# Gate-matrix operands in blocks of 8 tokens, one step ahead of their matmuls, and other rates for the gathered steps

## The chip, the core and the metric

The kernel runs on one core of a Trainium2 chip. A core has TensorE (PE in the rows), VectorE (DVE), ScalarE (ACT), GpSimd (POOL) and SyncE (SP), each with its own instruction queue, and DMA engines for moving data. The metric is the device time of one execution in microseconds, the median of several runs. A time inside the trace is counted from the start of the profiled span.

## The reference

One layer over 1024 tokens of width 1024: attention and mLSTM heads, then the product-key expert layer (PEER), then a gated projection and a norm. What matters here is PEER:

```python
# per token: 8 heads, each takes the 16 best of 128 x 128 experts
s = einsum('thcd,hcnd->thcn', q, sub_keys)          # scores of two halves of a key
sv, si = top_k(s, 16)                               # per half
cand = sv[..., 0, :, None] + sv[..., 1, None, :]    # 16 x 16 sums
top_s, pos = top_k(cand, 16); eidx = i * 128 + j    # of the chosen
g = softmax(top_s)
a = gelu(einsum('td,thkd->thk', x, expert_u[eidx]))
x = x + einsum('thk,thkd->td', g * a, expert_v[eidx])
# then, per token
x = x + sigmoid(rms_norm(x) @ w_ple_gate) * (p @ w_ple_proj);  out = rms_norm(x)
```

## The kernel before

The 1024 tokens are 8 tiles of 128. The kernel has four stretches: a front part (attention, mLSTM, projections and the choice of experts, to 974 us), dense_up (to 2009), dense_down (to 2932) and the tail (to 3122).

PEER is done in two ways. Tiles 0 to 2 fetch the rows of their 128 experts per token: `sparse` (L831) yields 400 steps, of which most hold a `u_step` (a gather of 512 KB by POOL at L827, then one VectorE multiply and sum, ru, L843) and a `v_step` (a gather of 512 KB and one VectorE addition onto ya, L861). After the last one of a tile, SP stores ya to x3_s (L865). `pump(x)` (L212) adds x to what is due and takes that many steps: `UP_RATE` says how many per column of dense_up (0.9 up to column 40, 1.45 from there), `DOWN_RATE` how many per row of dense_down (1.05, times a group of 4 rows), `TAIL_RATE` 8 at two places of each tail tile. A step's instructions get a lower priority than their surroundings, and each is kept behind the last VectorE operation that `anchor` (L201) has noted.

The other five tiles are done densely, against all 16384 experts. `dense_up` (L944) runs over 128 columns j: a table block of expert_u (raw, 512 KB) is split by ScalarE into thi and by VectorE into tlo (L881), TensorE makes A (L145), ScalarE ga (L992), which is stored to ga_s. `dense_down` (L1005) runs over 128 rows m in groups of four: it loads gq from g_s (L1049) and aq from ga_s (L1050), multiplies them (L1058), splits the product into ph and pl, and adds ph, pl times thi, tlo of expert_v into two kept PSUM banks (keep) and others (Y).

Between them stand the gates: `gate_blocks` (L891) makes, for the dense tiles, the 128 x 128 matrix of gate weights of each token as a product of two one-hot matrices, o0 (which first index) and o1 or w0 (which second index, times the weight in a high and a low part). For 16 tokens VectorE makes o1 (L918), w0 (L919), the low part in o1 (L920) and o0 (L921); for each 8 of them ScalarE copies w0 and o1 into wc in another order (L927), TensorE does 16 matmuls into pg (L931), ScalarE copies two pg into st (L934). For 32 tokens st, 2 MB, is stored to g_s (L938). The generator yields after each 8 tokens, 80 times in all. dense_up takes its steps (L999) from about column 42 on, at a pace that ends near column 119, and takes what is left after the last column (L1002). o0, o1, w0 and wc have one buffer each.

The tail (L1111) takes the tiles in the order 4, 0, 5, 6, 7, 1, 3, 2. A tile of 0 to 2 first pumps until its gathered sum is stored, then loads it as x (L1124), which TensorE transposes (L1139).

## Time and profile before

| | us |
|---|---|
| median of 3 runs | 3117.79 |
| lowest and highest run | 3115.04, 3124.81 |
| the profiled execution | 3123.69 |
| its span in the trace | 3121.9 |
| TensorE busy in the span | 2873.4 (92%) |
| VectorE busy in the span | 2557.4 (82%) |
| ScalarE, POOL busy in the span | 1317.8, 1007.6 |

In the rows of a later section, L12 is line 12 of the kernel before. "out<-in" gives the program's names of what an instruction writes and reads; o stands for o0 and o1, w for w0. An arrow in brackets says how long the engine was idle before, and what ended that. The granted clock is a share of TensorE's full speed. An instruction's duration in a row runs until its writes are done, and the next one of the same engine can start a little before that, so the cost of one instruction in a row of them is the distance between two starts.

### The profile page before, as it was taken

What the parts mean: (1) busy time and instruction counts of PE and PEld (TensorE: products, weight loads), DVE (VectorE), ACT (ScalarE), POOL (GpSimd) and SP (SyncE); (2) the same over time, 40 slices, a digit from 0 to 9 for tenths busy, and PEclk for the clock granted to TensorE, in tenths of its full rate; (3) what the DMA queues carried; (4) which work ended last, traced back from release to release, by engine and by line L of the source; (5) the groups of instructions that cost most, each with busy time, mean ns of one, the idle gap of its engine ahead of it and who ended that gap; (6) DMA issues with size and microseconds to landing.
All of it is one profiled execution on the core that took longest, in us unless ns stands there. A gap on an engine that the chain in (4) does not pass through costs nothing.

```text
span 3121.9 us, 44819 instructions
## 1 busy us (share of the span) xinstructions
PE 2873.4 (92%) x16367; PEld 2517.4 (81%) x16367; DVE 2557.4 (82%) x5349; ACT 1317.8 (42%) x2152; POOL 1007.6 (32%) x786
## 2 busy tenths in 40 slices
PE   7999989998697999999999999899989999998894
PEld 6887868776586999998889999778768888887773
DVE  5565889888799889799999797678778888888795
ACT  5664336655222222487776565212222222232241
POOL 0000000334414333444444555434333444414431
PEclk9999989999898999999999999899999999999997
DMA  5333433777846787899999989999989999988763
GB/s 168 100 111 127 150 126 93 233 229 244 303 133 233 264 276 244 306 345 340 343 340 346 370 328 367 372 348 340 313 291 330 339 333 329 338 295 276 259 222 124
DMA packets 316797, 829.01 MB, mean 266 GB/s; under 512 B 26144, under 2 KB 115104, under 8 KB 314016
## 3 DMA queue, kind: packets, MB, share of 16 engines
q0 software_dynamic: 112608, 410.04, 37.6%
q1 hardware_dynamic: 185536, 374.16, 34.9%
q10 hardware_dynamic: 18432, 41.95, 3.5%
q8 instruction: 128, 2.10, 0.3%
q14 instruction: 93, 0.76, 0.1%
HBM read 715.43 MB, written 102.24 MB: 262 GB/s over the span
## 4 chain that ended last, share of the span: by engine, by line
PE 55%; DVE 15%; DMA 12%; issue 12%; ACT 3%; POOL 2%; another core or an unknown queue 0%; SPq 0%; DVEq 0%; ACTq 0%; POOLq 0%
PE A L145 23%; PE mm L145 12%; PE keep L145 5%; DMA raw<-in_vr 4%; DMA rv<-in_ev,eidx 3%; DVE ya L861 3%; PE S L145 2%; DVE ru L843 2%; PE pg L931 2%; PE Y L136 2%; PE Y L137 2%; PE Y L138 2%; DVE tlo L881 1%; DMA ru<-in_eu,eidx 1%; POOL ru L827 1%
## 5 line engine op out<-in xcount | busy, mean ns | idle before, releaser
L827 POOL DMA_INDIRECT ru<-in_eu,eidx x384 | 508.4, 1324 | 1169.7 <-DVE ru L843 843.0
L827 POOL DMA_INDIRECT rv<-in_ev,eidx x384 | 491.2, 1279 | 443.5 <-DVE ya L861 286.8
L861 DVE SCALAR_TENSOR_TENSOR ya<-rv,cf,ya 128x1024 f32<-128x1024 f32 x384 | 492.3, 1282 | 46.5 <-DMA rv<-in_ev,eidx 29.3
L843 DVE SCALAR_TENSOR_TENSOR ru<-ru,sh 128x1024 f32<-128x1024 f32 x384 | 468.1, 1220 | 33.5 <-DMA ru<-in_eu,eidx 23.1
L881 DVE TENSOR_TENSOR tlo<-raw,thi 128x1024 fp32r<-128x1024 f32 x256 | 312.6, 1221 | 220.4 <-ACT thi L880 130.4
L880 ACT ACTIVATE thi<-raw 128x1024 fp32r<-128x1024 f32 x256 | 267.7, 1057 | 524.5 <-DMA raw<-in_vr 272.6
L145 PE MATMUL A<-ahi,thi 128*128 128x384 f32 x1024 | 348.7, 341 | 13.2 <-ACT thi L880 13.2
L145 PE MATMUL A<-alo,thi 128*128 128x384 f32 x1024 | 345.8, 338 | 0.0
L145 PE MATMUL mm<-ahi,whi 128*128 128x512 f32 (+1 forms) x752 | 301.4, 405 | 25.0 <-ACT ahi L236 13.1
L145 PE MATMUL mm<-alo,whi 128*128 128x512 f32 (+1 forms) x752 | 287.1, 394 | 7.1 <-DVE alo L237 7.1
L136 PE MATMUL Y<-thi,ph 128*128 128x512 f32 x640 | 250.2, 391 | 5.1 <-ACT thi L880 5.0
L145 PE MATMUL A<-xh,thi 128*128 128x256 f32 x1024 | 252.8, 284 | 0.7 <-ACT xh L971 0.7
L145 PE MATMUL A<-xl,thi 128*128 128x256 f32 x1024 | 252.7, 284 | 0.1
L137 PE MATMUL Y<-tlo,ph 128*128 128x512 f32 x640 | 250.0, 391 | 1.1 <-DVE tlo L881 1.0
L138 PE MATMUL Y<-thi,pl 128*128 128x512 f32 x640 | 249.4, 390 | 0.0
L1059 ACT ACTIVATE ph<-aq 128x640 fp32r<-128x640 f32 x128 | 87.3, 727 | 328.5 <-PE Y L137 309.4
L145 PEld LDWEIGHTS A<-ahi,thi 128*128 128x128 f32 x1024 | 193.6, 189 | 13.5 <-ACT thi L880 13.5
L145 PE MATMUL A<-ahi,tlo 128*128 128x384 f32 x1024 | 203.3, 337 | 0.0
L145 PE MATMUL keep<-tlo,ph 128*128 128x512 f32 x640 | 178.6, 403 | 22.7 <-DVE tlo L881 22.6
L145 PE MATMUL mm<-ahi,wlo 128*128 128x512 f32 (+1 forms) x752 | 193.9, 389 | 5.1 <-DVE wlo L196 5.0
L145 PEld LDWEIGHTS A<-xh,thi 128*128 128x128 f32 x1024 | 194.5, 190 | 1.0 <-ACT xh L971 0.9
L145 PEld LDWEIGHTS A<-xl,thi 128*128 128x128 f32 x1024 | 194.7, 190 | 0.3 <-DVE xl L972 0.3
(467 smaller groups left out, 6080.6 us busy)
## 6 DMA issues: line engine op xcount, KB each, us to landing
raw<-in_ut SPq DMA_DIRECT2D x128, 512.0 KB
raw<-in_vr SPq DMA_DIRECT2D x128, 512.0 KB
ga_s<-ga ACTq DMA_DIRECT2D x128, 320.0 KB
g_s<-st SPq DMA_DIRECT2D x20, 2048.0 KB
gq<-g_s SPq DMA_DIRECT2D x32, 1280.0 KB
aq<-ga_s SPq DMA_DIRECT2D x32, 1280.0 KB
wraw<-in_win SPq DMA_DIRECT2D x58, 512.0 KB
wraw<-in_wq SPq DMA_DIRECT2D x32, 512.0 KB
```

The costliest lines, as they stand in the source:

```text
L136: pe.matmul(o, lh, rh, start=start, stop=False)
L137: pe.matmul(o, lh, rl, start=False, stop=False)
L138: pe.matmul(o, ll, rh, start=False, stop=stop)
L145: pe.matmul(o, ll if p == "l" else lh, rl if p == "r" else rh, start=start and p == "h", stop=stop and n == last and p == names[-1])
L827: gp.indirect_dma_start(out=b, out_offset=None, in_=table, in_offset=bass.IndirectOffsetOnAxis(ap=eidx[part][:, i, k:k + 1], axis=0))
L843: behind(v.scalar_tensor_tensor(b, b, 1.0, st["h", tl], op0=OP.mult, op1=OP.mult, accum_out=st["d", n][:, j:j + 1]))
L861: op = v.scalar_tensor_tensor(ya, b, st["c", n][:, j:j + 1], ya, op0=OP.mult, op1=OP.add)
L880: sc.activation(hi, raw, AF.Copy)
L881: anchor(v.tensor_sub(lo, raw, hi.bitcast(F32)))
L931: pe.matmul(pg[:, b, :], o0[:, 4 * a + b, :], wc[:, c, a % 2, b, :], start=c == 0, stop=c == 1)
L1059: sc.activation(ph, av, AF.Copy)
```

## The change

Three numbers of the pace: `UP_RATE` takes 1.2 steps for each of the first 40 columns in place of 0.9, `DOWN_RATE` 1.1 in place of 1.05. And the gates: operands are made for 8 tokens at a time (o0, o1, w0 and each of the four VectorE operations have half the size), o0 and wc have two buffers, o1 and w0 still one. The matmuls, the copies to st and the store to g_s are in a function `gate_products`, which the generator calls for the operands of the step before, after it has emitted the operands of the current step. The last call stands behind the loop over tokens.

```diff
-UP_RATE = (0.9, 1.45, 40)
+UP_RATE = (1.2, 1.45, 40)
 QUIET = 5
-DOWN_RATE = 1.05
+DOWN_RATE = 1.1
...
-        sh = [P, 4, P, 4]
+        sh = [P, 2, P, 4]
         io = ioe[:, None].to_broadcast(sh)
+        prepared, held = [], {}
+
+        def gate_products(n, hb, sb, o0, wc):
+            if sb == 0:
+                held["st"] = gp_.tile([P, P, GB], F32, name="st", bufs=64 // GB)
+            st = held["st"]
+            for a in range(2):
+                pg = pG.tile([P, 4, P], F32, name="pg")
+                for b in range(4):
+                    for c in range(2):
+                        pe.matmul(pg[:, b, :], o0[:, 4 * a + b, :], wc[:, c, a, b, :], start=c == 0,
+                                  stop=c == 1)
+                t_ = sb * 8 + a * 4
+                sc.activation(st[:, :, t_:t_ + 4].rearrange("p j t -> p t j"), pg, AF.Copy, scale=1.0 / WSC)
+            if sb == GB // 8 - 1:
+                sy.dma_start(g_s[n * (P // GB) + hb], st)
+
...
-                st = gp_.tile([P, P, GB], F32, name="st", bufs=64 // GB)
-                for sb in range(GB // 16):
-                    tb = slice(hb * GB + sb * 16, hb * GB + sb * 16 + 16)
+                for sb in range(GB // 8):
+                    tb = slice(hb * GB + sb * 8, hb * GB + sb * 8 + 8)
...
-                    o0 = gp_.tile([P, 16, P], F16, name="o0", bufs=1)
+                    o0 = gp_.tile([P, 8, P], F16, name="o0", bufs=2)
                     o1 = gp_.tile(sh, F16, name="o1", bufs=1)
                     w0 = gp_.tile(sh, F16, name="w0", bufs=1)
-                    v.tensor_tensor(o1, iv[1], io, op=OP.is_equal)
-                    v.tensor_tensor(w0, o1, iv[2], op=OP.mult)
-                    v.tensor_tensor(o1, o1, iv[3], op=OP.mult)
-                    v.tensor_tensor(o0, it[:, 0, tb][:, :, None].to_broadcast([P, 16, P]),
-                                    ioe[:, None, :, 0].to_broadcast([P, 16, P]), op=OP.is_equal)
-                    for a in range(4):
-                        if a % 2 == 0:
-                            wc = gp_.tile([P, 2, 2, 4, P], F16, name="wc", bufs=1)
-                            for c, w in enumerate((w0, o1)):
-                                sc.activation(wc[:, c], w[:, a:a + 2].rearrange("p a j b -> p a b j"), AF.Copy)
...
-                        if a % 2:
-                            yield True
-                sy.dma_start(g_s[n * (P // GB) + hb], st)
+                    wc = gp_.tile([P, 2, 2, 4, P], F16, name="wc", bufs=2)
+                    v.tensor_tensor(o1, iv[0], io, op=OP.is_equal)
+                    v.tensor_tensor(w0, o1, iv[1], op=OP.mult)
+                    v.tensor_tensor(o1, o1, iv[2], op=OP.mult)
+                    for c, w in enumerate((w0, o1)):
+                        sc.activation(wc[:, c], w.rearrange("p a j b -> p a b j"), AF.Copy)
+                    v.tensor_tensor(o0, it[:, 0, tb][:, :, None].to_broadcast([P, 8, P]),
+                                    ioe[:, None, :, 0].to_broadcast([P, 8, P]), op=OP.is_equal)
+                    if prepared:
+                        gate_products(*prepared.pop())
+                    prepared.append((n, hb, sb, o0, wc))
+                    yield True
+        gate_products(*prepared.pop())
```

In the changed code the VectorE operations of a step are L935 (o1), L936 (w0), L937 (low part) and L940 (o0), the ScalarE copies to wc L939, the matmuls L907, the copies to st L910 and the store L912; gq and aq are loaded at L1057 and L1058.

VectorE within the gate stretch, in the order of the kernel before: from one block of 16 tokens to the next.

```order
L918 TENSOR_TENSOR o_15042<-it,ioe 128x2048
L921 TENSOR_TENSOR o_15041<-it,ioe 128x2048
L919 TENSOR_TENSOR w_15043<-o_15042,it 128x2048
L881 TENSOR_TENSOR tlo<-raw,thi 128x1024
L920 TENSOR_TENSOR o_15042<-o_15042,it 128x2048
L851 TENSOR_TENSOR cf<-cf,gsm_4438 128x16
L843 SCALAR_TENSOR_TENSOR ru,dots<-ru,sh_14973 128x1024
L861 SCALAR_TENSOR_TENSOR ya<-rv,cf,ya 128x1024 x2
L881 TENSOR_TENSOR tlo<-raw,thi 128x1024
L843 SCALAR_TENSOR_TENSOR ru,dots<-ru,sh_14973 128x1024
L918 TENSOR_TENSOR o_15298<-it,ioe 128x2048
```

The same place of the changed kernel: from one block of 8 tokens to the next, and the start of a third.

```order
L935 TENSOR_TENSOR o_14743<-it,ioe 128x1024
L940 TENSOR_TENSOR o_14837<-it,ioe 128x1024
L936 TENSOR_TENSOR w_14744<-o_14743,it 128x1024
L881 TENSOR_TENSOR tlo<-raw,thi 128x1024
L937 TENSOR_TENSOR o_14743<-o_14743,it 128x1024
L843 SCALAR_TENSOR_TENSOR ru,dots<-ru,sh_14405 128x1024
L861 SCALAR_TENSOR_TENSOR ya<-rv,cf,ya 128x1024
L935 TENSOR_TENSOR o_14838<-it,ioe 128x1024
L940 TENSOR_TENSOR o_15014<-it,ioe 128x1024
L936 TENSOR_TENSOR w_14839<-o_14838,it 128x1024
L843 SCALAR_TENSOR_TENSOR ru,dots<-ru,sh_14405 128x1024
```

Four operations of 2048 elements with eight others around them have become twice as many of 1024 elements, with fewer others in between: between the last use of o1 (L937) and its next writing (L935) stand two operations, where before L920 and L918 were six apart.

SP at the end of dense_up and the start of dense_down, before.

```order
L938 DMA g_s<-st 128x4096
L879 DMA raw<-in_ut 128x1024 x5
L938 DMA g_s<-st 128x4096
L879 DMA raw<-in_ut 128x1024 x4
L1049 DMA gq_20985<-g_s 128x20x128
L1050 DMA aq_20986<-ga_s 128x4x640
L879 DMA raw<-in_vr 128x1024 x2
L1049 DMA gq_20967<-g_s 128x20x128
```

The same place in the changed kernel.

```order
L912 DMA g_s<-st 128x4096
L879 DMA raw<-in_ut 128x1024 x8
L912 DMA g_s<-st 128x4096
L1057 DMA gq_21337<-g_s 128x20x128
L1058 DMA aq_21338<-ga_s 128x4x640
L879 DMA raw<-in_vr 128x1024 x2
L1057 DMA gq_21319<-g_s 128x20x128
```

The last store to g_s has moved from ahead of the last four loads of in_ut to a place behind them, directly ahead of the first gq.

VectorE near the end of the tail, before: the last ya, with the beginning of the last tile behind them (r_m, r_i and r_u are steps of its norm).

```order
L861 SCALAR_TENSOR_TENSOR ya<-rv,cf,ya 128x1024
L1182 SCALAR_TENSOR_TENSOR yac<-yac,r_u,gfin 128x512 x2
L861 SCALAR_TENSOR_TENSOR ya<-rv,cf,ya 128x1024 x5
L118 TENSOR_SCALAR r_m<-ss 128x1
L121 TENSOR_SCALAR r_m<-ss 128x1
L119 TENSOR_SCALAR r_i<-r_m 128x1
L120 TENSOR_SCALAR r_u<-r_i 128x1
L131 SCALAR_TENSOR_TENSOR r_h<-r_u,r_m 128x1
L1142 TENSOR_TENSOR al<-tr,ah 128x512
```

The last ya in the changed kernel, in the middle of another tile's work (yac and x are two tiles' outputs).

```order
L1182 TENSOR_TENSOR gt<-gt,pr 128x512
L1181 TENSOR_SCALAR gt<-gt 128x512
L1183 TENSOR_TENSOR x_28204<-gt,x_28204 128x512
L1182 TENSOR_TENSOR gt<-gt,pr 128x512
L861 SCALAR_TENSOR_TENSOR ya<-rv,cf,ya 128x1024
L1183 TENSOR_TENSOR x_28204<-gt,x_28204 128x512
L118 TENSOR_SCALAR r_m<-ss 128x1
L121 TENSOR_SCALAR r_m<-ss 128x1
L861 SCALAR_TENSOR_TENSOR ya<-rv,cf,ya 128x1024
L1186 TENSOR_TENSOR st_28337<-s_28325 128x1
L119 TENSOR_SCALAR r_i<-r_m 128x1
```

The last ya stands 184 rows ahead of the end there, before the last three tiles of the tail.

Over longer stretches of VectorE's order: by the end of column 40, 101 ru and 85 ya stand there before and 113 and 97 after; by the last tlo of dense_down 362 and 346 of 384 each before, 380 and 364 after. Between the tlo of columns 44 and 80 are 96 operations of the gates and 104 gathered ones before, 192 and 101 after; TensorE's order has the matmuls of 48 steps there in both.

## Rows read from the trace of the kernel before

**Rows 1.** Windows by stage: length, busy PE, PEld, DVE, ACT, POOL, clock, DMA, GB/s

```profile
974.00:1299.00 325.00, 321.29 (x2178) 319.63 (x2179) 286.32 (x864) 94.14 (x151) 122.87 (x94) 0.99 0.79 274
1299.00:1640.00 341.00, 316.25 (x2562) 303.26 (x2561) 312.70 (x313) 269.02 (x315) 144.16 (x108) 1.00 0.91 333
...
2009.00:2932.00 923.00, 885.93 (x3810) 726.63 (x3811) 750.50 (x955) 217.12 (x269) 343.87 (x265) 0.97 0.93 319
2932.00:3122.00 190.00, 133.00 (x575) 106.05 (x574) 141.12 (x354) 55.87 (x108) 59.27 (x50) 0.85 0.59 192
```

**Rows 2.** Timeline, last 44 us: start, duration, engine, line, [idle before <-what ended it]

```profile
3086.78 1.28 DVE L861 SCALAR_TENSOR_TENSOR ya<-rv,cf,ya 128x1024 f32<-128x1024 f32 x1 [1.13 <-DMA rv<-in_ev,eidx]
3088.09 0.33 SPq L865 DMA_DIRECT2D x_s<-ya  x1
3090.75 0.33 SPq L1124 DMA_DIRECT2D x<-x_s  x1
...
3093.98 1.97 PE L1139 MATMUL tr<-ident,x 128*128 128x128 f32 x8 [34.00 <-DMA x<-x_s]
```

**Rows 3.** Timeline of DVE: last tlo of dense_down, two tiles' st

```profile
2917.00 1.23 DVE L881 TENSOR_TENSOR tlo<-raw,thi 128x1024 fp32r<-128x1024 f32 x1 [1.25 <-ACT thi L880]
...
2983.78 0.16 DVE L1178 TENSOR_TENSOR st<-s 128x1 f32<-128x1 f32 x1
...
3026.44 0.15 DVE L1178 TENSOR_TENSOR st<-s 128x1 f32<-128x1 f32 x1
```

**Rows 4.** Timeline of ACT: ga after columns 4, 44, 80, 100, 104

```profile
1017.72 0.77 ACT L992 ACTIVATE ga<-A 128x384 f32<-128x384 f32 x2 [1.28 <-PE A L145]
...
1299.57 0.49 ACT L992 ACTIVATE ga<-A 128x384 f32<-128x384 f32 x1
...
1637.16 0.77 ACT L992 ACTIVATE ga<-A 128x384 f32<-128x384 f32 x2
...
1858.96 0.77 ACT L992 ACTIVATE ga<-A 128x384 f32<-128x384 f32 x2 [1.27 <-PE A L145]
...
1889.96 0.77 ACT L992 ACTIVATE ga<-A 128x384 f32<-128x384 f32 x2 [1.27 <-PE A L145]
```

**Rows 5.** Timeline of DVE inside the gate stretch

```profile
1401.80 2.29 DVE L921 TENSOR_TENSOR o<-it,ioe 128x2048 f16<-128x2048 f16 x1
1404.00 1.22 DVE L919 TENSOR_TENSOR w<-o,it 128x2048 f16<-128x2048 f16 x1
...
1407.41 1.22 DVE L843 SCALAR_TENSOR_TENSOR ru<-ru,sh 128x1024 f32<-128x1024 f32 x1
...
1408.55 1.28 DVE L861 SCALAR_TENSOR_TENSOR ya<-rv,cf,ya 128x1024 f32<-128x1024 f32 x1
1409.75 1.22 DVE L843 SCALAR_TENSOR_TENSOR ru<-ru,sh 128x1024 f32<-128x1024 f32 x1
```

**Rows 6.** Waits of DVE, 1299 to 1640: who <- whom: sum us, times, longest

```profile
DVE o L918 <- ACT wc L927: 14.1, 17, 1.8
DVE tlo L881 <- ACT wc L927: 3.6, 2, 2.2
...
DVE o L921 <- PE pg L931: 2.3, 6, 0.6
```

**Rows 7.** A slice of 20 us at dense_down's start, columns as in Rows 1

```profile
2000.00:2020.00 20.00, 11.03 (x40) 8.52 (x38) 12.22 (x14) 5.39 (x8) 11.35 (x10) 0.74 1.04 397
```

**Rows 8.** Waits of DVE, 1060 to 1299

```profile
DVE tlo L881 <- issue: 33.8, 13, 3.5
```

**Rows 9.** Timeline of PE, end of dense_up

```profile
2000.02 1.11 PE L145 MATMUL A<-xh,tlo 128*128 128x256 f32 x8
2008.95 2.50 PE L145 MATMUL keep<-thi,ph 128*128 128x512 f32 x5 [7.83 <-ACT ph L1059]
```

**Rows 10.** Groups by line, 1299 to 1940: shapes, count, busy, mean ns, idle before

```profile
L934 ACT ACTIVATE st<-pg 128x512 f32<-128x512 f32 x160 | 169.0, 1172 | 22.8 <-PE pg L931 21.4 <-issue 1.3
```

**Rows 11.** Chain of waits, 1995 to 2040: start, us, what

```profile
2010.19 14.79 DMA raw<-in_vr
```

More of the change, by code (lines that the diff above doesn't have):

```diff
@@ L909, in gate_blocks @@
             for hb in range(P // GB):
-                st = gp_.tile([P, P, GB], F32, name="st", bufs=64 // GB)
-                for sb in range(GB // 16):
-                    tb = slice(hb * GB + sb * 16, hb * GB + sb * 16 + 16)
+                for sb in range(GB // 8):
+                    tb = slice(hb * GB + sb * 8, hb * GB + sb * 8 + 8)
                     iv = [it[:, c, tb].rearrange("p (a b) -> p a b", b=4)[:, :, None, :].to_broadcast(sh)
-                          for c in range(4)]
-                    o0 = gp_.tile([P, 16, P], F16, name="o0", bufs=1)
+                          for c in range(1, 4)]
+                    o0 = gp_.tile([P, 8, P], F16, name="o0", bufs=2)
@@ L923, in gate_blocks @@
-                    for a in range(4):
-                        if a % 2 == 0:
-                            wc = gp_.tile([P, 2, 2, 4, P], F16, name="wc", bufs=1)
-                            for c, w in enumerate((w0, o1)):
-                                sc.activation(wc[:, c], w[:, a:a + 2].rearrange("p a j b -> p a b j"), AF.Copy)
-                        pg = pG.tile([P, 4, P], F32, name="pg")
-                        for b in range(4):
-                            for c in range(2):
-                                pe.matmul(pg[:, b, :], o0[:, 4 * a + b, :], wc[:, c, a % 2, b, :], start=c == 0,
-                                          stop=c == 1)
-                        t_ = sb * 16 + a * 4
-                        sc.activation(st[:, :, t_:t_ + 4].rearrange("p j t -> p t j"), pg, AF.Copy,
-                                      scale=1.0 / WSC)
-                        if a % 2:
-                            yield True
```

## The prediction

> **What bounds the kernel now.** I read the windows by stage first [rows 1]. In the two dense stages TensorE is nearly always busy: 321.3 of 325 us in the first columns of dense_up, 885.9 of 923 us in dense_down. Two stretches fall off: 1299 to 1640 us, in which the gate matrices are made (316.3 of 341, VectorE 312.7 busy as well), and the last 190 us, in which TensorE works 133.0. So the questions are what holds TensorE in those two stretches, and whether VectorE, which the change burdens, has room elsewhere.
>
> The end of the trace answers the first [rows 2]. The last gathered addition (ya, L861) starts at 3086.78, its sum goes out to x3_s and comes back (3088.09, 3090.75), and only then, at 3093.98, TensorE transposes the last tile, after 34.00 us without work. Everything else of the tail was through by 3059.98: the gathered experts of tile 2 end last. VectorE passes the last tlo of dense_down at 2917.00 [rows 3], and the order has 60 gathered operations (ru, ya) behind it: 169.8 us for 60, 2.8 us each, because they share VectorE with the tail's tiles.
>
> In the gate stretch TensorE and VectorE stop each other. Column 44 ends at 1299.57 and column 80 at 1637.16, 337.6 us for 36 columns [rows 4]. From column 4 (1017.72) to column 44, with no gate work, 40 columns took 281.9 us, 7.05 us each; of columns 100 to 104 (1858.96 to 1889.96, four columns with three gate steps, 31.0 us) that leaves 0.94 us for a gate step. TensorE's own work for 36 columns and the 48 gate steps that the order has there is 36 x 7.05 + 48 x 0.94 = 299 us. VectorE's own work, from one start to the next [rows 5]: the wide comparison L921 2.20 us (1401.80 to 1404.00); an operation of 1024 f32 elements 1.14 us (1407.41 to 1408.55), one of 2048 f16 elements the same by its equal duration of 1.22; a gathered pair (1407.41 to 1409.75) 2.34 us. That is 24 x (3 x 1.14 + 2.20) + 104 x 1.17 + 37 x 1.14 = 299 us too. Either engine alone would need 299 us, together they take 338: the loss of 39 us is handshake. VectorE's share of it is in its waits [rows 6], summed from 1299 to 1640: 14.1 us before L918, whose buffer the ScalarE copies wc still read, 3.6 us before tlo behind the same copies, 2.3 us before L921 behind the matmuls that read the old o0: 20.0 us.
>
> **The change part by part.**
>
> Tail, -36 us. By the order, 12 pairs more have passed VectorE by column 40, and 6 more by the end of dense_down: 24 gathered operations are left there, not 60. At 2.8 us each they end 67 us after 2917, near 2984, and with store and load (3088.09 to 3093.98 takes 5.9) near 2990. The last tile's transposes are wanted at 3060 at the latest, so the wait of 34.0 us goes whole, with 70 us to spare. What is late next is TensorE's own order of tiles: the one operation st (L1178) that VectorE does for each tile comes at 2983.78 and three tiles later at 3026.44, 14.2 us a tile [rows 3], with both engines near full. The last tile, alone, needed 28 us from 3093.98 to the end of the span; behind a busy neighbour its first half overlaps, and its matmuls no longer follow an idle stretch (in the slice with the idle time at 2000 us the granted clock was 0.74 [rows 7]). I count 2 us for that, and bounds of -30 (a new wait of a few us for VectorE) and -42 (the last tile overlaps more).
>
> First columns, +2 us. The 12 pairs cost VectorE 12 x 2.34 = 28 us. It is idle 325 - 286.3 = 38.7 us there [rows 1], 33.8 us of it ahead of tlo with nothing outstanding [rows 8]. So the pairs fit by the sum, but tlo must come in time for each column. The 24 gathers of 512 KB are 12.6 MB more in a stretch that moved 274 GB/s against 397 in a full slice [rows 1, 7]. Bounds 0 and +8 (the column that is short by the whole of its pair three times in ten).
>
> Gate stretch, -17 us. The halves are made one step ahead, with two buffers for o0 and wc: TensorE finds its operands there, and VectorE no longer waits for wc or the matmuls, -20.0 us. Against it: the same elements now take 48 x 4 operations in place of 24 x 4. A 128x1 operation takes 0.16 us [rows 3], of which 0.08 overlaps the next one (1407.41 + 1.22 against 1408.55 [rows 5]); so an operation costs some 0.08 beside its elements, 96 x 0.08 = 8 us, less the 3 gathered operations that leave the stretch (3.5 us): VectorE's bound rises from 299 to about 303. I take 3 us. Still in one buffer are o1 and w0: L935 of the next step must wait for the ScalarE copy of the last one, which has half the elements now, and in the order one or two operations (1.2 to 2.3 us) stand between L937 and the next L935, so this is mostly hidden; behind a waiting L935 stand tlo, for which TensorE waits, and the gathers. Bounds: -33 (all of the handshake gone, VectorE alone bounds at 303 to 305) and +3 (none gone, only the extra operations). The middle is nearest to the waits that the trace names.
>
> [...]
>
> Boundary to dense_down, +10 us. In the changed code the products of the last step come only behind the loop, after column 127. In the order, 16 pg matmuls stand between the last A and the first keep on TensorE, and on SP the last g_s store stands directly ahead of the first gq load, which needs it; before, the store went four raw loads earlier. In the trace TensorE's last A begins at 2000.02 and the first keep at 2008.95 after 7.83 us idle [rows 9]. In the changed code: matmuls 0.9, the second ScalarE copy st 1.2 behind the first (1172 ns each [rows 10]), so the store starts some 3 us after the last A. A store or load of 512 KB took 3088.09 to 3090.75 [rows 2], 2.7 us, of which 1.3 are bytes at 397 GB/s and 1.4 fixed. The 2.1 MB of g_s need 5.3 + 1.4 = 6.7, then gq and aq, 2.6 MB, 6.6 + 1.4 = 8.0, then the mult, ph and pl 1.5 us: first keep 19 us after the last A at the least, and 31 if the transfers share the queues with raw and the gathers by half. That is 12 to 23 us later. Part of it comes back: before, the next wait was for raw (14.79 us from 2010.19 [rows 11]), and those loads go on meanwhile. Up to 11 us returned makes the bounds +1 and +23; I take +10.
>
> dense_down, +2 us. DOWN_RATE brings 6 more pairs: 15 us of VectorE, which has 923 - 750.5 = 172 us idle [rows 1], and 12 gathers of 512 KB, 6.3 MB. The DMA share is 0.93 at 319 GB/s; if bytes alone bounded the stage, they would cost 20 us, but TensorE is at 96%, so I take 2, bounds 0 and +10.
>
> Sum: -36 + 2 - 17 + 10 + 2 = -39 us. The profiled execution took 3123.7 us (span 3121.9), so 3084.7 by it; the median of the runs, 3117.8, is 5.9 us lower: 3079 us.
>
> **The rivals.**
>
> The handshake stays: o1 and w0 in one buffer bind VectorE to ScalarE as before, "one step ahead" gains nothing, and the change doesn't do what it says. For it: 14.1 of the 20.0 us of waits stand before L918, which writes just that buffer. Against it: copies of half the size and operations in between. The gate term is then +3 or 0: 3079 + 17 to 20, about 3098 us.
>
> The handshake goes whole: the stretch falls to VectorE's bound of 303 to 305, -33 us: 3063 us. For it: o0 and wc get a full step of slack. Against: two engines each at 99% seldom mesh so.
>
> The other side, VectorE becomes the bound: each moved pair lands on the path where it is put. Price 12 x 2.34 + 6 x 2.34 = 42 us, with +3 in the gates and +10 at the boundary against -36 in the tail: +19, 3137 us. It decides once over 23 of those 42 us are on the path (36 - 10 - 3). Against it: the idle 38.7 and 172 us of VectorE in those very stages. For it: tlo's idle time may be spread so that each column has less than a pair's worth.
>
> **How the numbers follow.** The forecast 0.57, handshake stays 0.20, handshake goes whole 0.17, VectorE the bound 0.06. The forecast's own terms move by some 15 us to either side (gate and boundary the most), so 3079 has 3060 to 3098 about it; reaching to the two neighbours with their own boundary terms the range is 3050 to 3106. About 0.3%, 9 us, is what a measurement of this kernel can tell from no change: faster means under 3108, slower over 3127. Of the handshake case a tenth or two passes 3108, with the boundary at +23: faster 0.87, same 0.08, slower 0.05.
>
> **What would show it.** The tail: no wait of the last transposes for x from x_s, last ya near 2980. The gate stretch: columns 44 to 80 in 315 to 325 us, L935 waiting for wc under 5 us in all; if these waits stay above 14, the second case holds. The first columns: column 44 within 8 us of its old time, otherwise VectorE is the bound. The boundary: gq waiting for the last g_s, first keep 19 us or more after the last A; if it starts within 8 us, my term is wrong. It would all be wrong if the gathered sum still ended last.

## The result, and the profile after

The changed kernel takes 3096.32 us (median of 6 runs, 3091.09 to 3103.22) against 3120.06 us for the kernel before in the same comparison: a ratio of 0.9925, 95% interval 0.9909 to 0.9942. That is 23.7 us faster, where 39 had been forecast. The time lies inside the range, and some 15 us of the gain are missing. The profiled executions have spans of 3121.9 and 3098.4 us, 23.5 us apart, so they can be compared stage by stage.

The windows of the changed kernel (length; busy PE, PEld, DVE, ACT, POOL with counts; clock, DMA share, GB/s), with the stretches cut at its own columns, answer to [rows 1]:

```profile
974.00:1303.00 329.00, 324.79 (x2204) 322.88 (x2205) 315.57 (x911) 98.18 (x156) 152.25 (x121) 0.99 0.86 311
1303.00:1628.00 325.00, 310.56 (x2503) 298.83 (x2502) 307.25 (x396) 263.24 (x307) 136.03 (x102) 0.99 0.92 333
...
1989.00:2023.00 34.00, 0.14 (x1) 0.14 (x1) 6.02 (x9) 4.11 (x6) 9.52 (x10) 0.54 1.05 386
2023.00:2897.00 874.00, 841.29 (x3616) 686.11 (x3617) 727.08 (x928) 209.77 (x261) 344.27 (x258) 0.98 0.94 325
2897.00:3099.00 202.00, 174.11 (x769) 139.94 (x767) 139.23 (x345) 63.12 (x115) 32.66 (x29) 0.96 0.43 146
```

Two things stand out. In the tail TensorE now works 174 of 202 us, at 0.96 of its clock in place of 0.85. And there is a stretch of 34 us between dense_up and dense_down in which it does nothing while the DMA engines move 386 GB/s. The gate stretch took 324.5 us, from column 44 to column 80 by ScalarE's ga (compare [rows 4], 337.6 us); the last ga is column 127's:

```profile
1303.40 0.54 ACT L1000 ACTIVATE ga<-A 128x384 f32<-128x384 f32 x1
...
1627.93 0.76 ACT L1000 ACTIVATE ga<-A 128x384 f32<-128x384 f32 x2 [1.14 <-PE A L145]
...
1987.90 0.76 ACT L1000 ACTIVATE ga<-A 128x384 f32<-128x384 f32 x2 [6.25 <-PE A L145]
```

To see where time is won and lost I follow marks that every kernel has: ga of a column, the issue of the gq of groups 4, 8, 16 and 31 (of 0 to 31) on SP (a group's gq goes out when its buffer is free, so it marks the progress of dense_down) and the end. Each is the difference to the kernel before, in us, in the profiled executions. No edit touches what runs ahead of column 0, so what a kernel shows there (-3.0 to +1.7) is no effect of its change, and only differences down a column count:

| mark (time in the kernel before) | changed | e3 gates alone | e2 rates alone | e11 UP_RATE alone | e1 last step early | e4 = e1, DOWN_RATE 1.05 |
|---|---|---|---|---|---|---|
| column 0 (993.1) | +1.5 | -3.0 | +1.0 | -1.2 | +1.7 | +0.1 |
| column 44 (1299.6) | +3.8 | -0.7 | +1.0 | -1.2 | +4.1 | +2.5 |
| column 80 (1637.2) | -9.2 | -20.3 | -2.3 | -4.2 | -9.2 | -10.7 |
| column 126 (1994.1) | -13.3 | -24.3 | -5.6 | -7.7 | -11.7 | -13.2 |
| gq of group 4 (2068.7) | +4.9 | -7.4 | -4.4 | -7.5 | -10.9 | -12.8 |
| gq of group 8 (2160.8) | +12.7 | -7.4 | +3.2 | -6.7 | -2.8 | -11.8 |
| gq of group 16 (2399.7) | +5.5 | -11.5 | -2.9 | -17.7 | -11.3 | -23.1 |
| gq of group 31 (2809.1) | +11.4 | -10.8 | +1.5 | -15.2 | -6.4 | -24.0 |
| end of the span (3121.9) | -23.5 | -11.1 | -30.9 | -49.2 | -40.6 | -59.1 |

Down the first column: the first 44 columns cost 2.3 us, the gate stretch brings 13.1 and the columns behind it 4.0, the boundary (column 126 to group 4) costs 18.2, dense_down another 7.8 up to group 8, gives 7.3 back to group 16 and loses 5.9 again to group 31, and what follows, mostly the tail, brings 35.

At the boundary, TensorE of the changed kernel (timeline; compare [rows 9], 7.83 us idle) has its last 16 gate matmuls and then nothing for 34.09 us:

```profile
1986.76 1.11 PE L145 MATMUL A<-xh,tlo 128*128 128x256 f32 x8
1987.71 1.07 PE L907 MATMUL pg<-wc,o 128*128 128x128 f16 x16
2022.86 2.50 PE L145 MATMUL keep<-thi,ph 128*128 128x512 f32 x5 [34.09 <-ACT thi L880]
```

SP and VectorE show why: the g_s store goes out at 1990.52, the gq that needs it can only follow at 2001.22, aq behind it, and VectorE's first multiplication of dense_down waits 27.77 us for that transfer (SP's instruction that issues aq took 9.66 us itself):

```profile
1990.52 0.33 SPq L912 DMA_DIRECT2D g_s<-st  x1
2001.22 0.38 SPq L1057 DMA_DIRECT2D gq<-g_s  x1
2001.65 9.66 SPq L1058 DMA_DIRECT2D aq<-ga_s  x1
```

```profile
2019.53 2.29 DVE L1066 TENSOR_TENSOR aq<-aq,gq 128x640 f32<-128x640 f32 x3 [27.77 <-DMA aq<-ga_s]
```

In the gate stretch, the waits of VectorE (who waits for whom: sum, times, longest; compare [rows 6]):

```profile
DVE ru L843 <- DMA sh<-h_s: 6.4, 1, 6.4
DVE o L935 <- ACT wc L939: 4.9, 9, 0.7
DVE ya L861 <- DMA ya<-x_s: 2.3, 1, 2.3
DVE o L940 <- PE pg L907: 1.8, 3, 0.8
DVE tlo L881 <- ACT wc L939: 1.6, 2, 1.1
DVE tlo L881 <- issue: 0.3, 1, 0.3
```

The handshake of 20.0 us is down to 8.3. But 8.7 us are waits for sh and ya, the two loads with which the next gathered tile begins. That switch falls into this stretch in the kernel before too, where it cost 3.5 us of waiting:

```profile
DVE ru L843 <- DMA sh<-h_s: 3.5, 1, 3.5
```

Of the 325 us VectorE works 307.3, and only 0.3 of its idle time had nothing outstanding. TensorE still waits there for wc, 13.2 us in place of 21.6 (the changed kernel first):

```profile
PE pg L907 <- ACT wc L939: 13.2, 20, 5.8
```

```profile
PE pg L931 <- ACT wc L927: 21.6, 25, 2.1
```

In the tail the last gathered sum leaves at 3007.07, and the longest wait of a tile's transposes is for a dense tile's yac:

```profile
3007.07 0.33 SPq L865 DMA_DIRECT2D x_s<-ya  x1
```

```profile
PE tr L1147 <- DVE yac L1087: 1.6, 1, 1.6
```

### The profile page after: what moved, and what is told of

It reads as the page before. It is cut to its first block, busy times and chain, and to the rows that moved or that the text cites. A ratio compares the mean times of both kernels' runs of the same rounds, so it can differ in the third digit from the quotient of the medians.

```text
span 3098.4 us, 44984 instructions
## 1 busy us (share of the span) xinstructions
PE 2875.5 (93%) x16367; PEld 2519.1 (81%) x16367; DVE 2566.8 (83%) x5509; ACT 1317.9 (43%) x2152; POOL 1016.7 (33%) x786
## 5 line engine op out<-in xcount | busy, mean ns | idle before, releaser
L827 POOL DMA_INDIRECT ru<-in_eu,eidx x384 | 499.5, 1301 | 1061.8 <-DVE ru L843 765.4
L827 POOL DMA_INDIRECT rv<-in_ev,eidx x384 | 509.3, 1326 | 456.9 <-DVE ya L861 329.6
L861 DVE SCALAR_TENSOR_TENSOR ya<-rv,cf,ya 128x1024 f32<-128x1024 f32 x384 | 491.0, 1279 | 38.7 <-DMA rv<-in_ev,eidx 25.2
L145 PE MATMUL keep<-thi,ph 128*128 128x512 f32 x640 | 173.8, 394 | 37.9 <-ACT thi L880 34.1
L145 PEld LDWEIGHTS A<-alo,thi 128*128 128x128 f32 x1024 | 194.8, 190 | 0.0
## 6 DMA issues: line engine op xcount, KB each, us to landing
g_s<-st SPq DMA_DIRECT2D x20, 2048.0 KB, 10.2
gq<-g_s SPq DMA_DIRECT2D x32, 1280.0 KB, 10.7
```

Of the source, the lines that this page charges most:

```text
L145: pe.matmul(o, ll if p == "l" else lh, rl if p == "r" else rh, start=start and p == "h", stop=stop and n == last and p == names[-1])
L827: gp.indirect_dma_start(out=b, out_offset=None, in_=table, in_offset=bass.IndirectOffsetOnAxis(ap=eidx[part][:, i, k:k + 1], axis=0))
L861: op = v.scalar_tensor_tensor(ya, b, st["c", n][:, j:j + 1], ya, op0=OP.mult, op1=OP.add)
```

## Experiments: the boundary

e1_flush takes only the deferral of the last step back:

```diff
                     prepared.append((n, hb, sb, o0, wc))
+                    if (n, hb, sb) == (NDT - 1, P // GB - 1, GB // 8 - 1):
+                        gate_products(*prepared.pop())
                     yield True
-        gate_products(*prepared.pop())
```

> The changed kernel with one edit: the products of the very last gate step are emitted in that step itself and not behind the loop over columns, so that the last g_s store goes out near column 119, four raw loads ahead of the first gq. Theory: the chain last product, store of 2 MB, gq, aq at the boundary costs the changed kernel 26 us (TensorE is idle 34.09 us there, and tlo of row 16 in dense_down comes 12.5 us later than before although column 127 ended 13.4 us earlier). Without it the first keep should follow the last A by about 9 us as before, and the time should be about 3096 - 26 = 3070 us. Rival: the transfers queued at the boundary (gathers and raw loads) are the cost and the chain is only what shows; then TensorE still idles over 20 us there and the time stays within 6 us of 3096.

Measured: 3082.39 us, ratio 0.9868 (0.9837 to 0.9898) to the kernel before, 14 us under the changed kernel (spans: 17.1). TensorE of this kernel at the same place:

```profile
1998.26 2.50 PE L145 MATMUL keep<-thi,ph 128*128 128x512 f32 x5 [8.81 <-ACT thi L880]
```

The idle time is back to 8.8 us, so the chain is its cause and not the transfers that are queued there anyway. By the marks the boundary costs 0.8 us here (-11.7 to -10.9) against 18.2. The 26 us that I expected was too much: part of what I read as boundary in the rows up to 16 is lost later, in kernels with and without the chain (-10.9 to -2.8 here).

e3_gates has the new gates and the old rates:

```diff
-UP_RATE = (1.2, 1.45, 40)
+UP_RATE = (0.9, 1.45, 40)
-DOWN_RATE = 1.1
+DOWN_RATE = 1.05
```

> The changed kernel with the old rates (0.9 and 1.05), so the new gates alone. Theory: -13 in the gate stretch, -4 behind it, +26 at the boundary, tail as before with its 34 us wait (the whole end moves along with dense_down): 3120 + 9 = 3129 us, slower than before. Rival, boundary costs as forecast 10: about 3113 us, and if the wait of the tail swallows the boundary's loss (the gathered steps run on during it): 3105 us.

Measured: 3116.1 us, ratio 0.9983 (0.9968 to 0.9997), between the two rivals and not slower. The stretch from column 44 to 80 gains 19.6 us (the sum of the gate term alone, 17, was right), the rest of dense_up 4.0, and the boundary takes 16.9 of it, with 33.64 us without work on TensorE:

```profile
2011.37 2.50 PE L145 MATMUL keep<-thi,ph 128*128 128x512 f32 x5 [33.64 <-ACT thi L880]
```

So the chain costs the same with either rates, and the new gates alone are worth almost nothing as long as their last step is deferred.

## Experiments: the rates

e2_rates and e11_up_alone have the old gates:

```diff
-UP_RATE = (0.9, 1.45, 40)
+UP_RATE = (1.2, 1.45, 40)
-DOWN_RATE = 1.05
+DOWN_RATE = 1.1    (in e2_rates only)
```

> The kernel before with the two rates alone (1.2 and 1.1). Theory: the tail's wait of 34 us for the gathered sum goes (-36.6), the first columns cost 2, dense_down up to 12 for the six pairs: 3086 to 3096 us; the gate stretch (columns 44 to 80) takes 338 us as before, and the boundary keeps its 8 us wait. Rival: the earlier steps get in the way of VectorE and the tail's gain is eaten by them: 3110 us or more.

> The kernel before with UP_RATE 1.2 alone: old gates, DOWN_RATE 1.05. Theory: the tail's wait goes (about -34), the switch of the gathered tile no longer holds a tlo in dense_down (-8), the first columns cost about 1, and what DOWN_RATE 1.1 cost e2_rates (19 by e1 and e4) is not there: 3085 - 19 = 3066 us. Rival: with the old gates the cost of 1.1 is smaller, since the odd steps fall elsewhere: 3075 to 3085.

Measured: 3084.66 us for both rates (ratio 0.988, 0.9851 to 0.9909) and 3077.25 us for UP_RATE alone (0.9865, 0.9831 to 0.9898). UP_RATE alone is thus worth about 42 us, more than the whole change, and the two rates alone, a little better than the 3086 to 3096 expected, beat the changed kernel by 12 us: with its last step deferred, the new gate code costs more than it brings. The time of e11 lies in the rival's interval: by medians DOWN_RATE 1.1 costs 7 us with the old gates, by the two profiled executions 18 (the runs of e2_rates go from 3082.87 to 3092.84, and the profiled one is its longest; that of e11_up_alone is among its shortest). The size stays open for the old gates.

e4_flush_down asks the same with the new gates:

```diff
-DOWN_RATE = 1.1
+DOWN_RATE = 1.05
```

> As e1_flush, with DOWN_RATE back at 1.05 (36 gathered operations are left for the tail, not 24). Theory: the six additional pairs of dense_down are what makes the changed kernel fall back from 1 us behind the kernel before at row 48 to 13 us behind at row 127, through 15 us of VectorE and 6.3 MB of gathers; without them 6 to 12 us less than e1_flush, about 3061 us, and the gathered sum still ends 40 us ahead of its use in the tail. Rival: the drift has another cause (the order of transfers); then within 3 us of e1_flush.

Measured: 3062.92 us, ratio 0.981 (0.978 to 0.9841), 19.5 us under e1_flush, more than the 6 to 12 that were expected. The table of marks shows where: 7.1 of them between the gq of group 4 and that of group 8 (e1 loses 8.1 there, e4 1.0), 8.6 from group 8 to group 31. The rows of dense_down (0 to 127), each marked by the start of its tlo, show it closer: e1 is slower by 6.9 us from row 8 to row 16, by next to nothing from 16 to 48 (228.6 and 228.3 us) and by 9.5 from 48 to 112. So there are two costs, an event and, late in the stage, a drift.

## Experiments: event and drift in dense_down

The event lies between the gq of groups 6 and 7 of e1_flush, at rows 13 and 14. VectorE there (timeline; pl is L1069):

```profile
2107.67 1.23 DVE L843 SCALAR_TENSOR_TENSOR ru<-ru,sh 128x1024 f32<-128x1024 f32 x1 [5.12 <-DMA sh<-h_s]
...
2109.43 0.81 DVE L1069 TENSOR_TENSOR pl<-aq,ph 128x640 fp32r<-128x640 f32 x1
2110.16 1.22 DVE L881 TENSOR_TENSOR tlo<-raw,thi 128x1024 fp32r<-128x1024 f32 x1
```

The first ru of the third gathered tile waits 5.12 us for that tile's row block (sh has one buffer), and a yac addition, pl and the tlo of the next rows stand behind it in VectorE's queue. With 4.2 steps a group in place of 4.4 (e4_flush_down) the same ru comes behind a tlo that it doesn't hold, and waits for nothing:

```profile
2110.63 1.23 DVE L881 TENSOR_TENSOR tlo<-raw,thi 128x1024 fp32r<-128x1024 f32 x1 [3.86 <-ACT thi L880]
2111.78 1.22 DVE L843 SCALAR_TENSOR_TENSOR ru<-ru,sh 128x1024 f32<-128x1024 f32 x1
```

e6_noswitch takes that tile's two loads away:

```diff
             if j == 0 and k0 == 0:
-                st["h", tl] = rs.tile([P, D], F32, name="sh2", bufs=1)
-                gp.dma_start(st["h", tl], h2_s[tl])
+                if n == len(units) - PH:
+                    st["h", tl] = st["h", units[n - 1][0]]
+                else:
+                    st["h", tl] = rs.tile([P, D], F32, name="sh2", bufs=1)
+                    gp.dma_start(st["h", tl], h2_s[tl])
...
(the same for st["y", tl])
```

> e1_flush without the two loads with which the third gathered tile begins (its h row block and its residual; it goes on with those of the second tile, so its sums are of other data). Both have one buffer. Theory: in e1_flush the first ru of the third tile waits 5.1 us for the h load ahead of four pl and the tlo of a group, and that group (the seventh) takes 33 us where e4_flush_down and the kernel before take 27; so 6 to 9 us less than e1_flush, 3074 to 3076. Rival: the seventh group is long because of the loads and gathers queued there, not by this wait: within 3 us of 3082.

Measured: 3076.16 us (ratio 0.9858, 0.9839 to 0.9878), 6.2 under e1_flush, as expected, though the runs of either spread over 7 and 12 us, so the marks have to decide. Against e1_flush it is 4.9 us earlier at column 0 already, which is no effect of the edit, and 4.0 at the gq of group 4; at group 8 it is 9.6 earlier, so 5.6 us are the event (2 of them are lost again by group 31).

Two kernels part VectorE's time from the bytes. e5_halfdve:

```diff
+            w = ring.get("cols", D)
-            behind(v.scalar_tensor_tensor(b, b, 1.0, st["h", tl], op0=OP.mult, op1=OP.mult,
+            behind(v.scalar_tensor_tensor(b[:, :w], b[:, :w], 1.0, st["h", tl][:, :w], op0=OP.mult, op1=OP.mult,
...
-            op = v.scalar_tensor_tensor(ya, b, st["c", n][:, j:j + 1], ya, op0=OP.mult, op1=OP.add)
+            op = v.scalar_tensor_tensor(ya[:, :w], b[:, :w], st["c", n][:, j:j + 1], ya[:, :w], op0=OP.mult, op1=OP.add)
...
+                ring["cols"] = D // 2
```

> e1_flush with the gathered operations of dense_down done on half their columns (512 of 1024; the other halves of those products and sums are left out), all gathers as they are: some 150 us less of VectorE in the stage, the same bytes. e4_flush_down showed that the last 0.05 of DOWN_RATE cost 19 us. Theory: what a gathered pair costs in dense_down is VectorE's time in front of pl and tlo; then 10 to 25 us less than e1_flush, 3057 to 3072. Rival: it is the bytes of the gathers in competition with raw, gq and aq; then within 4 us of 3082.

e8_halfbytes:

```diff
-        gp.indirect_dma_start(out=b, out_offset=None, in_=table,
+        w = ring.get("cols", D)
+        gp.indirect_dma_start(out=b[:, :w], out_offset=None, in_=table if w == D else table.rearrange("e (a b) -> (e a) b", a=2),
...
+                ring["cols"] = D // 2
```

> e1_flush with gathers of half rows in dense_down (256 KB in place of 512; those steps use the first half twice, so their sums are of other data), VectorE's time as it was: 1024 columns per operation, for ru in two operations of 512. About 70 MB less in the stage. Theory bytes: the raw waits and with them 15 to 35 us of the stage go, 3047 to 3067. Theory VectorE: within 4 us of 3082, or a few us more for the added operations.

Measured: e5_halfdve 3067.4 us (0.983, 0.9798 to 0.9862; its runs spread from 3056.22 to 3077.2), e8_halfbytes 3027.98 us (0.9705, 0.9685 to 0.9725), 19 us below the best that was expected. The time of e5 lies in the interval of the VectorE theory, so the times alone don't decide between the two.

Where the 17.5 us lie that the profiled execution of e5 is shorter than that of e1 does: 3.2 ahead of column 0 (no effect of the edit), 4.5 where the event was (group 6 to 8: from -3.7 to -8.2, in e6_noswitch from -3.7 to -9.6), 3.0 between groups 8 and 31 and 7.1 in the last rows, between the gq of group 31 and the last tlo.

Half the bytes bring 54 us. They don't come evenly: -12.3 us at group 4, -25.2 at 8, -39.0 at 16, -46.1 at 31, so most of it at the start of dense_down and at the places where a wait for a transfer stands. The drift by itself is read from rows 48 to 112, in which no tile is switched. The tlo of these two rows in e1_flush, in e4_flush_down and in e8_halfbytes:

```profile
2350.30 1.22 DVE L881 TENSOR_TENSOR tlo<-raw,thi 128x1024 fp32r<-128x1024 f32 x1
...
2796.02 1.23 DVE L881 TENSOR_TENSOR tlo<-raw,thi 128x1024 fp32r<-128x1024 f32 x1 [0.63 <-ACT thi L880]
```

```profile
2341.20 1.22 DVE L881 TENSOR_TENSOR tlo<-raw,thi 128x1024 fp32r<-128x1024 f32 x1
...
2777.44 1.22 DVE L881 TENSOR_TENSOR tlo<-raw,thi 128x1024 fp32r<-128x1024 f32 x1
```

```profile
2314.97 1.22 DVE L889 TENSOR_TENSOR tlo<-raw,thi 128x1024 fp32r<-128x1024 f32 x1
...
2750.43 1.23 DVE L889 TENSOR_TENSOR tlo<-raw,thi 128x1024 fp32r<-128x1024 f32 x1 [1.60 <-ACT thi L888]
```

That is 445.7, 436.2 and 435.5 us. In e1 four pairs more pass in these rows than in e4 (71 and 67 ya), so the drift is 2.4 us a pair. Half the bytes take it back whole; half the VectorE work (443.3 us in e5) takes back a quarter. A window of 300 us out of these rows, e1_flush first, then e8_halfbytes:

```profile
2400.00:2700.00 300.00, 297.47 (x1301) 243.12 (x1300) 257.50 (x329) 70.96 (x88) 126.81 (x95) 1.00 0.96 336
```

```profile
2400.00:2700.00 300.00, 300.00 (x1325) 248.43 (x1324) 271.92 (x438) 73.74 (x91) 123.22 (x98) 1.00 0.81 261
```

In e8_halfbytes TensorE is full and VectorE busier than ever (272 of 300), the DMA share 0.81. In e1_flush the DMA engines are at 0.96, and ScalarE waits for raw before thi; its sums in the two kernels from 2000 to 2890:

```profile
ACT thi L880 <- DMA raw<-in_vr: 295.1, 64, 16.4
```

```profile
ACT thi L888 <- DMA raw<-in_vr: 176.8, 63, 15.5
```

VectorE itself waits for gathered rows only 5.0 us in this stage of e1 (from 2020 to 2800 no such wait is listed), so its standing behind late gathers is not how the bytes act. The drift at this rate is thus for the most part bytes, although TensorE is counted busy 99% of the time.

## Experiments: how far the rates go

e7_down100 (e1_flush with `DOWN_RATE = 1.0`):

> e1_flush with DOWN_RATE 1.0 (about 50 gathered operations left for the tail in place of 24). Theory that each pair moved out of dense_down is worth its 3 us wherever it was: 3063 - 19 = 3044 us, as far as the gathered sum is ready in time (50 x 2.8 us after the last tlo is about the time at which the last tile wants it). Rival: the 19 us between 1.1 and 1.05 are mostly the places at which the switch of the gathered tile and the odd step fall among pl and tlo; then 3058 to 3068, and the tail may wait again.

Measured: 3056.24 us (0.9803, 0.9785 to 0.982), 7 under e4_flush_down, far from the theory and just under the rival's 3058. At group 31 it is 15 us ahead of e4 (-32.6 against -17.6 to e1_flush). Spread over the pairs that were moved (0.2 in each of 31 groups, 6.2 pairs) that would be 2.4 us a pair again, but it doesn't come by the pair: 10.9 us lie between rows 16 and 48 and 3.5 between 48 and 112. In the first of these stretches the third gathered tile's first ya stands. ya has one buffer, so the second tile's sum must be stored and the third's loaded before it. In the changed kernel, with 4.4 steps a group, VectorE and behind it TensorE stand there:

```profile
2243.82 1.28 DVE L861 SCALAR_TENSOR_TENSOR ya<-rv,cf,ya 128x1024 f32<-128x1024 f32 x1 [10.50 <-DMA ya<-x_s]
```

```profile
2246.29 2.50 PE L145 MATMUL keep<-tlo,ph 128*128 128x512 f32 x5 [6.63 <-DVE tlo L881]
```

In e4_flush_down the two waits are 10.24 and 6.22 us. With 4 steps a group the switch falls on the end of a group, pl and tlo come between the two ya, and in e7_down100 the wait is gone:

```profile
2222.78 1.28 DVE L861 SCALAR_TENSOR_TENSOR ya<-rv,cf,ya 128x1024 f32<-128x1024 f32 x1 [0.75 <-DMA ya<-x_s]
```

So most of it lies where the rival put it, at the place of the switch. At the last tlo e7 is 20.9 us ahead of e4, at the end 9.3: the rest is paid in the tail, where the last tile waits again, 4.8 us of it for x:

```profile
PE tr L1148 <- DMA x<-x_s: 4.8, 1, 4.8
```

e9_late160 and e10_up130 look for another place for those pairs. The first adds 0.15 to the rate from column 84 on and sets DOWN_RATE to 0.95; the second sets UP_RATE's first number to 1.3.

> e7_down100 with 0.15 steps more per column from column 84 on (1.60, 6 or 7 pairs) and DOWN_RATE 0.95 (as many pairs fewer in dense_down). Theory: dense_down pays some 2.4 us per pair in bytes (e4 and e7 after the seventh group), while columns 84 to 127 are bound by TensorE with 48 us of VectorE to spare; so about 15 us less, 3040 us. Rival: those columns move 353 to 367 GB/s already, as near to the 397 of a full slice as dense_down is, and the raw loads of in_ut would then come late: the gain is lost there, 3052 to 3062.

> e7_down100 with UP_RATE 1.3 in the first 40 columns (4 pairs more there, 4 fewer gathered pairs for the tail, where e7 waits 4.8 us for x). Theory: VectorE has 13 us to spare in these columns, 4 pairs take 9.4, so column 44 comes up to 3 us later and the wait of the tail goes: 3050 to 3055. Rival: VectorE has become the bound there, each pair costs its 2.34 us and shifts the switch of the gathered tile: 3060 or more.

Measured: 3056.24 us for e9_late160 (0.9799, 0.9782 to 0.9815), the same as e7_down100 and in the rival's interval, but not for the rival's reason. The columns are not slower (354.5 us from column 80 to 126 in both), TensorE is still full, and they move 389 GB/s at a DMA share of 1.00 (second row below), where e7_down100 has 0.97 (first row): the added pairs cost nothing there.

```profile
1626.00:1987.00 361.00, 360.27 (x2753) 358.75 (x2752) 312.05 (x388) 206.15 (x266) 192.28 (x141) 1.00 0.97 367
```

```profile
1626.00:1987.00 361.00, 359.81 (x2739) 358.13 (x2738) 326.27 (x408) 205.78 (x266) 211.83 (x156) 1.00 1.00 389
```

The gain is lost in dense_down, which is 4.9 us earlier at group 8 and 2.8 later at group 31. With 3.8 steps a group the waits of the switch are back (another of 4.39 us, for sh, comes before these):

```profile
2185.16 1.28 DVE L861 SCALAR_TENSOR_TENSOR ya<-rv,cf,ya 128x1024 f32<-128x1024 f32 x1 [9.38 <-DMA ya<-x_s]
```

```profile
2187.63 2.50 PE L145 MATMUL keep<-tlo,ph 128*128 128x512 f32 x5 [5.33 <-DVE tlo L881]
```

And three pairs fewer in rows 48 to 112 bring nothing any more (436.0 us against 432.8 in e7). The tail waits for x as before.

e10_up130 takes 3048.31 us, ratio 0.9774 (0.9758 to 0.9791), a little better than expected, and beats both kernels. Its first 44 columns take as long as those of e7_down100 to within 1 us, since VectorE had the room (13.4 of 329 us idle there in the changed kernel; four pairs at 2.34 us [rows 5] take 9.4), and the wait for x is down to 1.0 us. The gate stretch, of which nothing was expected, takes 321.0 us in place of 327.3.

e12_oldgates is e10_up130 with the old gates:

> The old gates with the rates of e10_up130 (1.3 and 1.0), so e10_up130 less the new gates. Theory: the gates bring what columns 44 to 80 show, 10 to 13 us, and some 3 behind them: 3048 + 10 to 16 = 3058 to 3064 us. Rival: the gates bring nothing that the end sees (the medians of e1_flush and e2_rates are only 2 us apart): 3046 to 3052.

Measured: 3067.9 us (0.9834, 0.9803 to 0.9865), 19.6 above e10_up130, more than the 10 to 16 expected. Column 126 ends at 1995.0 here and at 1975.4 there; 2.9 us of these 19.5 lie ahead of column 0 and 16.7 in dense_up, and the difference stays to the end. With the deferral of the last step gone, the new gates are worth the whole of what they save in dense_up.

All kernels side by side, by the stretch in which the third tile's ya stands, by its wait for the load, and by the stretch without a switch (us, profiled executions):

| kernels | DOWN_RATE | rows 16 to 48 | wait of ya | rows 48 to 112 |
|---|---|---|---|---|
| before, e3 (UP_RATE 0.9) | 1.05 | 239.3, 237.3 | 13.3, 12.4 | 438.0, 436.4 |
| e11, e4 | 1.05 | 228.4, 228.3 | 10.9, 10.2 | 440.6, 436.2 |
| changed, e2, e1 | 1.1 | 230.1, 230.9, 228.6 | 10.5, 11.2, 10.4 | 446.7, 445.4, 445.7 |
| e7, e10, e12 | 1.0 | 217.4, 217.2, 217.6 | 0.8, 0.4, 0.1 | 432.8, 434.7, 434.2 |
| e9 | 0.95 | 223.7 | 9.4 | 436.0 |
| e5 (half VectorE) | 1.1 | 227.2 | 10.7 | 443.3 |
| e8 (half bytes) | 1.1 | 216.1 | 4.7 | 435.5 |

(e6_noswitch has no such load; its ya waits 6.35 us for the store, and the stretches take 227.4 and 449.1 us.) The last column shows that a pair has no fixed price: from 1.05 to 1.1 the mean rises by some 8 us, from 1.0 to 1.05 by 4, from 0.95 to 1.0 not at all.

## Why the prediction was right or wrong

The forecast was 39 us less, and the profiled executions differ by 23.5. Of the 15.5 that are missing 8.2 lie at the boundary, 6.2 in dense_down, 3.9 in the gate stretch and 1.5 ahead of column 0, where nothing was changed; the columns 80 to 126 gave 4.0 that no term had.

**Tail, -36: right.** From the last tlo (2917.00 and 2930.1) to the end it took 204.9 us before and 168.3 after, 36.6 less. The wait of 34.00 us is gone whole, and the clock of the stretch rose to 0.96, one of the two things for which the two further us were put; no run parts them. The gathered sum is stored at 3007.07, 77 us after the last tlo and not 67.

**First columns, +2: the number right by luck.** It was +2.3, but not for the pairs. Columns 0 to 40 take 277.6 us in the kernel before and in the changed kernel alike, and with the old gates and UP_RATE 1.2 (e2_rates, e11_up_alone) the first 44 columns cost nothing at all. The 2.3 us lie in columns 40 to 44, where the gates begin, and e3_gates has them with the old rate. VectorE's idle time held the 12 pairs whole; its busy time went from 286.3 of 325 to 315.6 of 329 us.

**Gate stretch, -17: right for the gates, off by 4 in this kernel.** Alone (e3_gates) they bring 19.6, and 13.1 in the changed kernel. The step that was missing is the switch of the gathered tile, whose place the rates move: 8.7 us of waits for sh and ya stand in this stretch of the changed kernel, 2.6 in e3_gates. The one buffer of o1 and w0, of which the rival "the handshake stays" made its case, costs 4.9 us. Halving the operations cost about what was worked out (0.08): two starts of half-size operations are 0.60 us apart (1422.03 to 1422.63 below) and full-size ones took 1.14 (1400.66 to 1401.80, L918 in the kernel before), so 0.06 each. By the durations it would be 0.16 (twice 0.69 against 1.22), but 0.09 of the 0.69 us overlap the next operation.

```profile
1422.03 0.69 DVE L936 TENSOR_TENSOR w<-o,it 128x1024 f16<-128x1024 f16 x1
1422.63 1.22 DVE L940 TENSOR_TENSOR o<-it,ioe 128x1024 f16<-128x1024 f16 x1
1423.77 0.69 DVE L937 TENSOR_TENSOR o<-o,it 128x1024 f16<-128x1024 f16 x1
```

**Boundary, +10: the mechanism was right, the size too small.** It cost 18.2 (e3_gates: 16.9; e1_flush without the chain: 0.8). The first keep comes 36.1 us after the last A, outside the 19 to 31 that had been worked out (8.9 before, by [rows 9], so these would have been 10 to 22 later and not 12 to 23): from the issue of the store to the issue of gq passed 10.7 us where I had put 6.7, and aq landed 17.9 us after its issue began where I had put 8.0 for both loads; 9.66 of the 17.9 went by in the issuing instruction itself. The price of a transfer alone was taken from a pair of rows in the quiet end of the kernel (71 GB/s from 3078 to 3122, DMA share 0.21); here the gathers and raw shared 386 GB/s. TensorE's idle time grew by 26.3 us and the boundary by 18.2, so 8 came back, as the bounds had it.

**dense_down, +2: the step that failed.** From group 4 to the last tlo the stage lost 8.2 us, inside the bounds of 0 to 10, but as the difference of two larger things. The six pairs of DOWN_RATE cost 19.5 us with the new gates (e1_flush against e4_flush_down; 18.6 from row 0 to the last tlo), over the bound of 10. The prediction put bytes aside because TensorE was busy 96% of the time; the drift of 9.5 us in rows 48 to 112 and e8_halfbytes show that this was no reason. That its "if bytes alone bounded the stage, they would cost 20 us" lies next to 19.5 is chance: some 7 us are the event of the tile switch, which no term had. And the place of the next switch gave some 9 us back (239.3 to 230.1 us from row 16 to 48), which no term had either. Before, the ya of the third tile waited 13.31 us for its load, ahead of pl and a tlo for which TensorE stood 10.1 us:

```profile
2323.82 1.28 DVE L861 SCALAR_TENSOR_TENSOR ya<-rv,cf,ya 128x1024 f32<-128x1024 f32 x1 [13.31 <-DMA ya<-x_s]
2325.02 0.82 DVE L1060 TENSOR_TENSOR pl<-aq,ph 128x640 fp32r<-128x640 f32 x1
2325.76 1.22 DVE L881 TENSOR_TENSOR tlo<-raw,thi 128x1024 fp32r<-128x1024 f32 x1
```

```profile
2327.03 2.50 PE L145 MATMUL keep<-tlo,ph 128*128 128x512 f32 x5 [10.10 <-DVE tlo L881]
```

With UP_RATE 1.2 that wait comes twelve rows earlier and is shorter, 10.50 and 6.63 us in the changed kernel, and with DOWN_RATE 1.0 it is gone. So between the gq of groups 8 and 16 e3_gates, with the old rate, gains 4 us on the kernel before, the kernels with UP_RATE 1.2 and DOWN_RATE 1.05 or 1.1 gain 6 to 12, and those with DOWN_RATE 1.0 gain 21 to 22. No run moves this switch alone. That the wait is the cause rests on the kernels of the table, above all on e9_late160, which has the fewest pairs, the wait and a longer stretch than the three without it.

**The columns named 100 and 104** in the prediction and in [rows 4] are 108 and 112; the four columns between them and the 31.0 us are as stated, so nothing in the sum changes.

**The rivals.** "VectorE becomes the bound" did not come: the pairs cost nothing in the first columns, and in dense_down their price at the highest rate is for the most part in bytes (2.4 us a pair), near its 2.34 us by chance. In the gate stretch VectorE has no room left (0.3 us), but TensorE's wait for wc is still there as well. The handshake neither stayed nor went whole.

## What to carry to other kernels

Software pipelining has an end: where the last deferred piece heads a chain of store, load and use, flush it inside the loop, or the next stage starts late by the whole chain (here 17 us, nearly what the pipelining had won). A change with several parts should be measured against its parts: here the two rates alone are faster than the whole. When a stage shows a busy TensorE and nearly full DMA engines, neither number says what one more transfer costs: here a pair of gathers cost 2.4 us at the highest rate of dense_down, about half of that or nothing at lower ones, and nothing in columns 84 to 127, with the DMA share at 1.00. Take the price from runs that differ in bytes alone, over a stretch without other waits. And where a paced side task has single buffers at its seams, a rate also decides which instructions stand behind the wait at the seam; look for those places before and after.

## What the runs showed of the hardware

Under the load of this boundary (1.05 of the DMA engines' share, 386 GB/s) a store of 2 MB held its dependent load back for 10.7 us, and a load of 1.25 MB landed 17.9 us after its issue began, of which SP's issuing instruction took 9.66; in the quiet end of the tail (71 GB/s, DMA share 0.21) the load of a sum of 512 KB was issued 2.7 us after its store [rows 2]. Of the stretches over 100 us whose rows stand here, the 361 us of e9_late160 moved the most, 389 GB/s, with TensorE busy for 359.8 us of them at a granted clock of 1.00. On VectorE, operations of 1024 and of 2048 f16 elements (o1, w0 and the low part) started 0.60 and 1.14 us apart, so two halves cost 0.06 us more than the whole; o0 took 1.14 and 2.20 us, almost twice as long at either size.
